# Attention in a hybrid decoder block: the product of weights and values taken by query halves, with the masked weights' high and low parts stacked

## The chip, the core and the metric

The kernel runs on one core of a Trainium2 chip. Its engines work side by side, each through its own list of instructions in order: TensorE (PE in the profile; its weight loads are listed as PEld), VectorE (DVE), ScalarE (ACT), GpSimd (POOL) and SyncE (SP, which here only issues DMA transfers; POOL issues some too). The metric is the device time of one execution, in microseconds (us).

## The reference

One residual block on a sequence of 1024 tokens and 1024 channels, float32. A normalised input is projected to query, key, value, gates and a recurrent branch; both branches are gated, projected, merged, projected once more and added to the input. Only the attention is touched here. It has 16 heads of 64 channels in 4 groups that share key and value, a window of 128 keys, and a learned sink per head:

```python
qb = q.reshape(B, nb, BLOCK, N_KV_HEADS, G, hd)        # BLOCK = 128
kb = jnp.concatenate([kp[:, :-1], kp[:, 1:]], axis=2)  # block before, own block
vb = jnp.concatenate([vp[:, :-1], vp[:, 1:]], axis=2)
diff = qi + BLOCK - kj
band = (diff >= 0) & (diff < WINDOW)                   # WINDOW = 128
s = jnp.where(mask, s, -1e30)
p = jnp.exp(s - m)
denom = jnp.sum(p, axis=-1, keepdims=True) + jnp.exp(sink - m)
o = jnp.einsum('bnkgqs,bnskd->bnqkgd', p / denom, vb)
```

A query at place q of its block sees the keys 0 to q of its own block and the keys q+1 to 127 of the block before. So for each query there is exactly one visible key at each place 0 to 127, and 128 weights hold all of a row's softmax.

## The kernel before

Float32 products are made from rounded parts: an operand is split into a high part, rounded to a shorter format (`F32R`), and a low part, the rest; high times high, high times low and low times high are summed in PSUM. A cast on ACT makes the high part, a subtraction on DVE the low one. TensorE multiplies a loaded 128x128 stationary operand with a moving operand of up to 512 columns.

**The attention works in 32 units u**: group g = u // 8, block n = u % 8, four heads of 128 queries each. One unit goes through these steps, which a loop over u (at the end of the kernel, ahead of `del W["att"]`) spreads over four rounds:

- `sink(u)`: POOL copies the four sinks into a tile `p` (three buffers) of 4 x 129 columns.
- `scores(u)` (L1330): PE, eight products of 256 columns (128 for n = 0) into `s_ps`, one buffer in PSUM.
- `maxima_a`, `maxima_d`: ACT copies the own block's scores to `p`, DVE overwrites them where the mask says so by the block before (L1345; for n = 0 POOL masks instead, L1348), and DVE takes the row maxima into `small` (L1350).
- `weights_a`, `weights_d`, one round later: ACT exponentials with their sums (L1355), DVE divides by the sums (L1361, L1362).
- `transposed`, `split_a`, `split_d`, `masks`, two rounds later: PE turns `p` to keys on partitions (`pt`, L1369), ACT casts the high part `phc` (L1374), DVE makes the low part `plc` (L1380), POOL zeroes in both the keys after the query, giving `phm` and `plm` (L1389).
- `values`, `join_a`, `join_d`, three rounds later: PE multiplies (L1403), ACT and DVE add the halves of the result into `yq` (L1412, L1413, L1423, L1424).

With w the transposed weights, v' the block before's values and v the own block's, the output is w times v' plus mask(w) times (v - v'). The stationary tile `vd` has v' (or v - v') with its high part in columns 0 to 63 and its low part in columns 64 to 127. So `values` takes four products of 512 columns: `phc` and `plc` with v', `phm` and `plm` with v - v'. A unit with n = 0 has only the first two.

**Who prepares what.** `v_prep(g)` builds these value tiles once per group, long before the attention, and stores them to DRAM (`vd_d`) with two transfers from POOL's queue. `load_v(m)` fetches them, 256 KB for two units, also from POOL's queue, into two buffers.

**What sets the order.** PE, ACT, DVE, POOL and SP run an order that the program writes out by hand. In each round PE does `scores(u)`, one piece of other work (12 products of 512 columns, from the projection of the recurrent branch: `rp`, L173, and in the first rounds the end of the input projection, `bk`, L709), `transposed(u-2)`, `values(u-3)`. ACT does the copy for `maxima_a(u)`, `weights_a(u-1)`, other casts, `split_a(u-2)`, `join_a(u-3)`. DVE follows the same pattern, with `weights_d(u-1)`, `split_d(u-2)`, `join_d(u-3)`, gating steps of finished pairs of units (L1538, L1548), the low parts of the weights of `rp` (L111). The piece of work on `rp` needs the recurrent branch's output from DRAM (`yh`, `yl`), which SP's queue fetches in the same stretch.

**Where tiles lie.** The attention's tiles are in pools on the right side of the on-chip memory that are opened one below the other: `yo` (`ob`, `yq`, and two tiles `phm`, `plm` of 2 KB in each partition), below it `pp` (a filler `pad`, three `p` of 2064 bytes, placed 2080 bytes apart, and four `small`), below it `at` (two `vd` of 2 KB, `phc`, `plc`). Within a pool, the tile asked for first lies lowest. The space was the recurrent branch's before; a tile's first use waits for whoever still reads or stores what lay there. The last such tile is `it`, the low part of the last channel block, which POOL's queue stores to `yl_d` (512 KB) as the attention begins.

Of the kernel before, what the change touches and what calls it, by code (L numbers as in the profile page):

```python
# [12 lines left out]
F32 = mybir.dt.float32  # L13
F32R = mybir.dt.float32r
# [4 lines left out]
ALU = mybir.AluOpType  # L19
# [3 lines left out]
P = 128  # L23
# [3 lines left out]
HALF = 512  # L27
NH = 16
NG = 4
# [19 lines left out]
KEEP_BUSY = 4  # L49
SLACK = 1.0, 1.3, -1.0  # L50
BANKS = (0, 1, 2, 3), (4, 5, 6, 7)


@with_exitstack
def tile_hybrid_block(ctx, tc, x, pk, rows, posr, posi, c_row, w_ss, w_gate, w_main, w_v,
                      w_g, w_ap, w_rp, w_out, out):
    nc = tc.nc
    V, A, G, T = nc.vector, nc.scalar, nc.gpsimd, nc.tensor

    def dma(dst, src, eng=nc.sync):  # L60
        dst, src = (a.bitcast(F32) if a.dtype == F32R else a for a in (dst, src))
        return eng.dma_start(dst, src)  # L62

    def f32(ap):
        return ap.bitcast(F32)
# [4 lines left out]
    def pool(st, name, bufs=1, **kw):  # L70
        return st.enter_context(tc.tile_pool(name=name, bufs=bufs, reuse_waits="tile", **kw))
# [14 lines left out]
    ident = const.tile([P, P], F32, name="ident")  # L86
# [43 lines left out]
    vd_d = [tc.dram_tile([P, 8, 2, P], F32, name=f"vd_d{g}") for g in range(NG)]  # L130
# [60 lines left out]
    with ExitStack() as st:  # L191
# [11 lines left out]
        for i in range(8):  # L203
            t = sp.tile([P, D], F32, tag="xt", name="xt", bufs=XT)
# [214 lines left out]
        def turn(n=100):  # L419
            for _ in range(n):  # L420
                if next(angle, 0) == 0:
# [10 lines left out]
                    out=bng[:], in0=pk_t[:, PK_BSC:PK_BSC + 8], scalar=1.0,  # L432
                    in1=pk_t[:, PK_NG:PK_NG + 8], op0=ALU.add, op1=ALU.mult)]}
# [133 lines left out]
    def make_operands(i):  # L567
        nl = hx.tile([P, 2, S], F32R, tag="X", name="nl")
        for a in range(2):
# [8 lines left out]
    W = {}  # L578
# [11 lines left out]
                    channel_multiplier=-1)  # L590
# [57 lines left out]
    class Load:  # L648

        pe = act = dve = 0.0  # L650
# [503 lines left out]
    def v_prep(g):  # L1154
        t = {}
        vpp = W["vpp"]

        def f0():
            t["v"] = vpp.tile([P, 8, 64], F32, tag="v32", name="v32")
            dma(t["v"][:], v_d[:, :, g, :], G)  # L1160

        def f1():
            t["d"] = vpp.tile([P, 8, 64], F32, tag="d32", name="d32")
            V.tensor_tensor(out=t["d"][:, 1:8, :], in0=t["v"][:, 1:8, :],
                            in1=t["v"][:, 0:7, :], op=ALU.subtract)
# [24 lines left out]
    def w_out_gate():  # L1190
# [88 lines left out]
    at = psx = None  # L1279
    U = {}  # L1280

    def open_attn():
        nonlocal at, psx
        psm_ctx.close()
        psx = pool(psx_ctx, "psx", space=PSUM)
        W["kq", 1] = pool(at_ctx, "kq1", side="right")
        W["yo"] = pool(at_ctx, "yo", side="right")
        W["pp"] = pool(at_ctx, "pp", bufs=3, side="right")
        W["pp"].tile([P, 72], F32, name="pad", bufs=1)
        at = pool(at_ctx, "at", side="right")  # L1290
        load_kq(1)
        load_v(0)

    def load_kq(m):
        g, t0 = m // 4, (m % 4) * 256
# [18 lines left out]

    def sink(u):
        px = U["p", u] = W["pp"].tile([P, 4, P + 1], F32, tag="p", name="p")
# [47 lines left out]

    def transposed(u):
        px = U.pop(("s", u))[1]
        pt = psx.tile([P, 4, P], F32, tag="t", name="pt")
        for j in range(4):
            W["pe"] = T.transpose(pt[:, j, :], px[:, j, 0:P], ident[:])  # L1369
        U["t", u] = [pt]  # L1370

    def split_a(u):
        phc = at.tile([P, 4, P], F32R, tag="phc", name="phc")
        A.copy(phc[:], U["t", u][0][:])  # L1374
        U["t", u].append(phc)

    def split_d(u):
        pt, phc = U.pop(("t", u))
        plc = at.tile([P, 4, P], F32R, tag="plc", name="plc")
        V.tensor_tensor(out=plc[:], in0=pt[:], in1=f32(phc[:]), op=ALU.subtract)  # L1380
        U["m", u] = phc, plc

    def masks(u):
        phc, plc = U["m", u]
        ms = []
        if u % 8:
            for s_, tag in ((phc, "phm"), (plc, "plm")):
                d_ = W["yo"].tile([P, 4, P], F32R, tag=tag, name=tag)
                G.affine_select(out=d_[:], in_=f32(s_[:]), pattern=[[0, 4], [1, P]],  # L1389
                                compare_op=ALU.is_ge, fill=0.0, base=0,  # L1390
                                channel_multiplier=-1)
                ms.append(d_)
        U["m", u] = [phc, plc], ms

    def values(u):
        n = u % 8
        vd = U["v", u // 2]
        full, masked = U.pop(("m", u))
        prods = [(vd[:, n % 2, 1 if n else 0, :], m) for m in full]
        prods += [(vd[:, n % 2, 0, :], m) for m in masked]  # L1400
        pv = psx.tile([P, 4 * P], F32, tag="v", name="pv")
        for i, (b, m) in enumerate(prods):
            W["pe"] = T.matmul(pv[:], b, m[:].rearrange("p j q -> p (j q)"),  # L1403
                               start=(i == 0), stop=(i == len(prods) - 1))
        U["pv", u] = [pv[:].rearrange("p (a e q) -> p a e q", a=2, e=2)]
        if n % 2 == 0 and u // 2 + 1 < 16:
            load_v(u // 2 + 1)

    def join_a(u):
        pvv = U["pv", u][0]  # L1410
        ob = W["yo"].tile([P, 2, P], F32, tag="ob", name="ob")
        A.copy(ob[0:64], pvv[64:128, :, 0, :])  # L1412
        A.copy(ob[64:128], pvv[0:64, :, 1, :])  # L1413
        U["pv", u].append(ob)

    def join_d(u):
        g, n = u // 8, u % 8
        pvv, ob = U.pop(("pv", u))
        if n % 2 == 0:
            W["yq"] = W["yo"].tile([P, 2, 256], F32, tag="yq", name="yq", bufs=3)  # L1420
            U["yq", u // 2] = W["yq"]
        yo = W["yq"][:, :, (n % 2) * P:(n % 2 + 1) * P]
        V.tensor_tensor(out=yo[0:64], in0=pvv[0:64, :, 0, :], in1=ob[0:64], op=ALU.add)  # L1423
        V.tensor_tensor(out=yo[64:128], in0=pvv[64:128, :, 1, :], in1=ob[64:128], op=ALU.add)  # L1424


    ps_ctx = ExitStack()
# [266 lines left out]
    for u in range(32 + 3):  # L1694
# [101 lines left out]
    for c in range(KC):  # L1796
# [24 lines left out]
        if c < 4:  # L1821
            h, l = A11[c]
# [87 lines left out]
    t_ = [tpool.tile([P, 2, 2, HALF], F32R, tag="T", name="s2") for _ in range(2)]  # L1910
# [42 lines left out]
    f = fs[:, 7, :]  # L1953

    def square_d(sl, acc):
# [17 lines left out]
                           in1=fg_bc[:, LEFT], op0=ALU.mult, op1=ALU.mult)  # L1973
# [5 lines left out]
                           in1=fg_bc[:, LEFT], op0=ALU.mult, op1=ALU.mult)  # L1979
# [80 lines left out]
```

## Time and profile before

| | |
|---|---|
| median of 3 runs | 906.73 us (906.5 to 907.61) |
| the profiled execution's own time | 907.17 us |
| its span, first to last instruction | 905.5 us |
| PE busy | 895.4 us (99%) |
| DVE busy | 717.1 us (79%) |
| ACT busy | 567.4 us (63%) |
| POOL busy | 124.7 us (14%) |
| attention on PE, first scores to last values | 557.8 to 730.1 us |
| granted clock | 0.999 |

A busy PE is not a PE at its peak: the profile's records of one product overlap with the next, so the pace of products is read from the distance between their starts. Idle time of an engine that is off the chain costs nothing. Times inside the span count from its first instruction; 1.67 us of the execution lie outside.

### The profile page before, as it was taken

To read this page: it belongs to the slowest core of one execution; us is meant where nothing else is said; L and a number is where in the kernel's file an instruction comes from. 1 tells how busy PE (TensorE), PEld (TensorE's weight loads), DVE (VectorE), ACT (ScalarE), POOL (GpSimd) and SP (SyncE) were. 2 spreads that over 40 slices of the span, in tenths; PEclk is the share of its full clock that TensorE was granted. 3 is DMA by queue.
4 is the path that set the end of the run, shared out by engine and by line. 5 is a ranking of instruction groups with operands and counts; after the bars stand their busy time and mean duration, and the time that the engine had idled before them with its cause. 6 is when DMAs were issued, how large, how long until landed. Compare 5 with 4: busy or idle time off the path is not lost.

```text
span 905.5 us, 12654 instructions
## 1 busy us (share of the span) xinstructions
PE 895.4 (99%) x4258; PEld 746.2 (82%) x4259; DVE 717.1 (79%) x1073; ACT 567.4 (63%) x1098; POOL 124.7 (14%) x216
## 2 busy tenths in 40 slices
PE   9999999999999999999999999999999999999997
PEld 6789888888888888888888888888888888888886
DVE  6987688988669875987788597999989846578855
ACT  7965554654566855786485884888888732115535
POOL 6520251200000000000000002343443300000000
PEclk9999999999999999999999999999999999999999
DMA  9829489772435353354446367996655289416604
GB/s 355 339 69 286 164 258 319 256 235 95 151 128 180 123 209 135 125 183 162 157 144 213 105 201 242 344 401 217 214 202 203 83 306 367 140 47 232 209 1 186
DMA packets 87349, 180.74 MB, mean 200 GB/s; under 512 B 8642, under 2 KB 29138, under 8 KB 87284
## 3 DMA queue, kind: packets, MB, share of 16 engines
q1 hardware_dynamic: 83200, 167.07, 52.5%
q0 software_dynamic: 3936, 12.59, 4.4%
q8 instruction: 34, 0.56, 0.3%
q14 instruction: 31, 0.25, 0.1%
q10 hardware_dynamic: 148, 0.27, 0.1%
HBM read 121.34 MB, written 58.95 MB: 199 GB/s over the span
## 4 chain that ended last, share of the span: by engine, by line
PE 52%; issue 42%; DVE 3%; ACT 2%; DMA 1%; POOL 0%; DVEq 0%; ACTq 0%; POOLq 0%
PE rp L173 14%; PE bk L709 10%; PE out L1863 6%; PE pmain L173 5%; PE s_ps L1330 3%; PE pv L1403 3%; PE pmain L485 2%; PE bk L485 2%; PE pt L1369 1%; DMA yl_d<-it 1%; PE pmain L1579 1%; PE pmain L1580 1%; PE pmain L1578 1%; ACT jk L1881 1%; PE bk L256 1%
## 5 line engine op out<-in xcount | busy, mean ns | idle before, releaser
L709 PE MATMUL bk<-nh,wh 128*128 128x512 f32 x368 | 143.4, 390 | 0.0
L709 PE MATMUL bk<-nl,wh 128*128 128x512 f32 x368 | 143.3, 389 | 0.0
L709 PE MATMUL bk<-nh,wl 128*128 128x512 f32 x368 | 98.4, 389 | 0.0
L111 DVE TENSOR_TENSOR wl<-r,wh 128x512 fp32r<-128x512 f32 x109 | 74.8, 692 | 23.3 <-ACT wh L105 23.2
L105 ACT CAST wh<-r 128x512 fp32r<-128x512 f32 x107 | 65.6, 618 | 32.1 <-PE rp L173 11.8
L709 PEld LDWEIGHTS bk<-nh,wl 128*128 128x128 f32 x368 | 69.1, 188 | 14.3
L709 PEld LDWEIGHTS bk<-nh,wh 128*128 128x128 f32 x368 | 69.2, 188 | 14.2
L709 PEld LDWEIGHTS bk<-nl,wh 128*128 128x128 f32 x368 | 69.1, 188 | 14.1
L709 PE MATMUL bk<-hh,wh 128*128 128x512 f32 x184 | 71.7, 390 | 0.0
L709 PE MATMUL bk<-hl,wh 128*128 128x512 f32 x184 | 71.6, 389 | 0.0
L111 DVE TENSOR_TENSOR wl<-ws,wh 128x512 fp32r<-128x512 f32 x76 | 52.1, 686 | 7.2 <-ACT wh L105 7.1
L62 POOL DMA_DIRECT2D yh_d<-av x1 | 0.6, 567 | 371.9 <-ACT av L1092 371.9
L1355 ACT ACTIVATE p<-p,small 128x129 f32<-128x129 f32 x128 | 50.0, 396 | 0.0
L709 PE MATMUL bk<-hh,wl 128*128 128x512 f32 x184 | 49.2, 389 | 0.0
L105 ACT CAST wh<-ws 128x512 fp32r<-128x512 f32 x76 | 46.0, 614 | 4.8 <-DVE ws L731 2.4
L709 PEld LDWEIGHTS bk<-hh,wl 128*128 128x128 f32 x184 | 34.6, 188 | 7.1
L709 PEld LDWEIGHTS bk<-hh,wh 128*128 128x128 f32 x184 | 34.6, 188 | 7.1
L709 PEld LDWEIGHTS bk<-hl,wh 128*128 128x128 f32 x184 | 34.6, 188 | 7.1
L1330 PEld LDWEIGHTS s_ps<-ks,qs 128*128 128x128 f32 x256 | 34.1, 189 | 4.4 <-DVE p L1345 2.0
L1330 PE MATMUL s_ps<-ks,qs 128*128 128x256 f32 (+1 forms) x256 | 35.6, 282 | 0.3 <-DVE p L1345 0.2
L709 PE MATMUL bk<-hha,wh 128*128 128x512 f32 x92 | 35.8, 390 | 0.0
L709 PE MATMUL bk<-hla,wh 128*128 128x512 f32 x92 | 35.8, 389 | 0.0
(378 smaller groups left out, 2293.1 us busy)
## 6 DMA issues: line engine op xcount, KB each, us to landing
r<-w_main SPq DMA_DIRECT2D x100, 256.0 KB, 4.2
wada<-w_ss SPq DMA_DIRECT2D x16, 512.0 KB, 9.0
qs<-q_d SPq DMA_DIRECT2D x16, 512.0 KB, 5.2
wo_d<-wr SPq DMA_DIRECT2D x28, 256.0 KB, 3.1
wo<-wo_d SPq DMA_DIRECT2D x14, 512.0 KB, 5.6
ks<-k_d SPq DMA_DIRECT2D x12, 384.0 KB, 4.3
xt<-x SPq DMA_DIRECT2D x8, 512.0 KB, 7.1
sma_d<-c SPq DMA_DIRECT2D x16, 256.0 KB, 4.4
```

The costliest lines, as they stand in the source:

```text
L105: A.copy(dst[0][:], src)
L111: V.tensor_tensor(out=dst[1][:], in0=src, in1=f32(dst[0][:]), op=ALU.subtract)
L173: mm = T.matmul(ps[hf], ww, xx[kc][hf], start=(kc == 0 and ww is w_h and xx is xh), stop=(kc == KC - 1 and xx is xl))
L256: T.matmul(bk[i % 2], zero[:, 0:P], zero, start=True, stop=True)
L485: T.matmul(starts[c][hf], ww[:, c0:c0 + P], xh[kc][hf], start=(kc == 0 and t_ == "h"), stop=(kc == KC - 1 and t_ == "l"))
L709: W["pe"] = T.matmul(ps, ww[:, kc * P:(kc + 1) * P], b[kc][i], start=(first and n == 0), stop=(n == 11), skip_group_check=not first)
L1330: W["pe"] = T.matmul(o, qs[:, j, qc], ks[:, kb:n % 2 + 2, b, :], start=(b == 0), stop=(b == 1))
L1355: A.activation(px[:, j, :], px[:, j, :], AF.Exp, bias=sm[:, 0, j:j + 1], accum_out=sm[:, 1, j:j + 1])
L1369: W["pe"] = T.transpose(pt[:, j, :], px[:, j, 0:P], ident[:])
L1403: W["pe"] = T.matmul(pv[:], b, m[:].rearrange("p j q -> p (j q)"), start=(i == 0), stop=(i == len(prods) - 1))
L1578: T.matmul(o, hh[kc][th][:, ts_], wh[:, cols], start=(kc == 0), stop=False)
L1863: T.matmul(o, a[k][x_][:, p * P:(p + 1) * P], b[k][y_][:, cols], start=(first and k == 0 and i == 0), stop=(k == 3 and i == 2), skip_group ...
```

## The change

By halves of 64 queries, the mask gets smaller. For queries 0 to 63, the keys 64 to 127 of the own block are always masked; for queries 64 to 127, the keys 0 to 63 are never masked. So:

- the transposed weights are laid out by query half, then head (`p l j q`); the transposes write two runs of 64 columns each;
- for half 0 the plain product uses v'; for half 1 its stationary tile has v in the rows of keys 0 to 63 and v' in those of keys 64 to 127;
- only 64 keys are left under the mask in either half. Their high part takes 64 partitions of a tile `pm`, their low part the other 64, against a stationary tile that has v - v' of these keys twice;
- `values` takes three products of 256 columns per half, six in all, for four of 512 (units with n = 0 keep their two of 512);
- `masks` makes four POOL instructions of 64 partitions x 256 columns for two of 128 x 512, two of which move data to the other 64 partitions;
- `v_prep` stores more and in smaller parts: eight transfers per group for two, some 1.9 MB for 0.96 MB; `load_v` now fetches 256 KB for each unit, two units ahead, into three buffers;
- one tile `pm` takes the place of `phm` and `plm`; the joins read and write runs of 64 columns for runs of 128.

```diff
@@ v_prep, f3
-            dma(vd_d[g][:, 1:8, 1, :], t["vs"][:, 0:7, :], G)
-            dma(vd_d[g][:, :, 0, :], t["dv"][:], G)
+            o, vs, dv = vd_d[g], t["vs"], t["dv"]
+            dma(o[:, 1:8, 0, 0, :], vs[:, 0:7, :], G)
+            dma(o[:, 0, 0, 0, :], vs[:, 0, :], G)
+            dma(o[TOP, 1:8, 1, 0, :], vs[TOP, 1:8, :], G)
+            dma(o[END, 1:8, 1, 0, :], vs[END, 0:7, :], G)
+            for l, half_ in enumerate((TOP, END)):
+                for to in (TOP, END):
+                    dma(o[to, 1:8, l, 1, :], dv[half_, 1:8, :], G)
@@ open_attn
         load_v(0)
+        load_v(1)
@@
-    def load_v(m):
-        g, n0 = m // 4, (m % 4) * 2
-        vd = at.tile([P, 2, 2, P], F32R, tag="vd", name="vd", bufs=2)
-        if n0:
-            dma(vd[:], vd_d[g][:, n0:n0 + 2, :, :], G)
+    def load_v(u):
+        g, n = u // 8, u % 8
+        vd = U["v", u] = at.tile([P, 2, 2, P], F32R, tag="vd", name="vd", bufs=3)
+        if n:
+            dma(vd[:], vd_d[g][:, n, :, :, :], G)
         else:
-            dma(vd[:, 0, 0, :], vd_d[g][:, 0, 0, :], G)
-            dma(vd[:, 1, :, :], vd_d[g][:, 1, :, :], G)
-        U["v", m] = vd
+            dma(vd[:, 0, 0, :], vd_d[g][:, 0, 0, 0, :], G)
@@ transposed
-        pt = psx.tile([P, 4, P], F32, tag="t", name="pt")
+        pt = psx.tile([P, 2, 4, 64], F32, tag="t", name="pt")
         for j in range(4):
-            W["pe"] = T.transpose(pt[:, j, :], px[:, j, 0:P], ident[:])
+            W["pe"] = T.transpose(pt[:, :, j, :], px[:, j, 0:P], ident[:])
@@ masks
-            for s_, tag in ((phc, "phm"), (plc, "plm")):
-                d_ = W["yo"].tile([P, 4, P], F32R, tag=tag, name=tag)
-                G.affine_select(out=d_[:], in_=f32(s_[:]), pattern=[[0, 4], [1, P]],
-                                compare_op=ALU.is_ge, fill=0.0, base=0,
-                                channel_multiplier=-1)
+            pm = W["yo"].tile([P, HALF], F32R, tag="pm", name="pm")
+            lo, hi = slice(0, 256), slice(256, HALF)
+            for to, s_, from_, cols in ((TOP, phc, TOP, lo), (END, phc, END, hi),
+                                        (END, plc, TOP, lo), (TOP, plc, END, hi)):
+                G.affine_select(out=pm[to, cols], in_=f32(s_[from_, cols]),
+                                pattern=[[0, 4], [1, 64]], compare_op=ALU.is_ge, fill=0.0,
+                                base=0, channel_multiplier=-1)
@@ values
-        prods = [(vd[:, n % 2, 1 if n else 0, :], m) for m in full]
-        prods += [(vd[:, n % 2, 0, :], m) for m in masked]
-        for i, (b, m) in enumerate(prods):
-            W["pe"] = T.matmul(pv[:], b, m[:].rearrange("p j q -> p (j q)"),
-                               start=(i == 0), stop=(i == len(prods) - 1))
+        for l in range(2 if n else 1):
+            cols = slice(l * 256, l * 256 + 256) if n else slice(0, HALF)
+            for i, t_ in enumerate(m):
+                W["pe"] = T.matmul(pv[:, cols], vd[:, l, i // 2, :], t_[:, cols],
+                                   start=(i == 0), stop=(i == len(m) - 1))
@@
-        if n % 2 == 0 and u // 2 + 1 < 16:
-            load_v(u // 2 + 1)
+        if u + 2 < 32:
+            load_v(u + 2)
@@ join_a, join_d (operands in runs of 64, same elements)
-        A.copy(ob[0:64], pvv[64:128, :, 0, :])
+        A.copy(ob[0:64], pvv[64:128, :, :, 0, :])
...
```

More of the change, by code (lines that the diff above doesn't have):

```diff
@@ L51 @@
 BANKS = (0, 1, 2, 3), (4, 5, 6, 7)
+TOP, END = slice(0, 64), slice(64, 128)
 @with_exitstack
@@ L129, in tile_hybrid_block @@
     v_d = tc.dram_tile([P, 8, NG, 64], F32, name="v_d")
-    vd_d = [tc.dram_tile([P, 8, 2, P], F32, name=f"vd_d{g}") for g in range(NG)]
+    vd_d = [tc.dram_tile([P, 8, 2, 2, P], F32, name=f"vd_d{g}") for g in range(NG)]
     q_d = [tc.dram_tile([4, 512, 256], F32, name=f"q_d{g}") for g in range(NG)]
@@ L1366, in transposed @@
         px = U.pop(("s", u))[1]
-        pt = psx.tile([P, 4, P], F32, tag="t", name="pt")
+        pt = psx.tile([P, 2, 4, 64], F32, tag="t", name="pt")
         for j in range(4):
-            W["pe"] = T.transpose(pt[:, j, :], px[:, j, 0:P], ident[:])
-        U["t", u] = [pt]
+            W["pe"] = T.transpose(pt[:, :, j, :], px[:, j, 0:P], ident[:])
+        U["t", u] = [pt[:].rearrange("p l j q -> p (l j q)")]
     def split_a(u):
-        phc = at.tile([P, 4, P], F32R, tag="phc", name="phc")
-        A.copy(phc[:], U["t", u][0][:])
+        phc = at.tile([P, HALF], F32R, tag="phc", name="phc")
+        A.copy(phc[:], U["t", u][0])
         U["t", u].append(phc)
@@ L1378, in split_d @@
         pt, phc = U.pop(("t", u))
-        plc = at.tile([P, 4, P], F32R, tag="plc", name="plc")
-        V.tensor_tensor(out=plc[:], in0=pt[:], in1=f32(phc[:]), op=ALU.subtract)
+        plc = at.tile([P, HALF], F32R, tag="plc", name="plc")
+        V.tensor_tensor(out=plc[:], in0=pt, in1=f32(phc[:]), op=ALU.subtract)
         U["m", u] = phc, plc
@@ L1395, in values @@
+            lo, hi = slice(0, 256), slice(256, HALF)
[4 more added lines that the diff above has]
+                                base=0, channel_multiplier=-1)
+            U["m", u] = phc, plc, pm
     def values(u):
@@ L1396, in values @@
         n = u % 8
-        vd = U["v", u // 2]
-        full, masked = U.pop(("m", u))
-        prods = [(vd[:, n % 2, 1 if n else 0, :], m) for m in full]
-        prods += [(vd[:, n % 2, 0, :], m) for m in masked]
+        vd = U.pop(("v", u))
+        m = U.pop(("m", u))
         pv = psx.tile([P, 4 * P], F32, tag="v", name="pv")
-        for i, (b, m) in enumerate(prods):
-            W["pe"] = T.matmul(pv[:], b, m[:].rearrange("p j q -> p (j q)"),
-                               start=(i == 0), stop=(i == len(prods) - 1))
@@ L1409, in join_a @@
+        if u + 2 < 32:
+            load_v(u + 2)
     def join_a(u):
         pvv = U["pv", u][0]
-        ob = W["yo"].tile([P, 2, P], F32, tag="ob", name="ob")
-        A.copy(ob[0:64], pvv[64:128, :, 0, :])
-        A.copy(ob[64:128], pvv[0:64, :, 1, :])
+        ob = W["yo"].tile([P, 2, 2, 64], F32, tag="ob", name="ob")
+        A.copy(ob[0:64], pvv[64:128, :, :, 0, :])
+        A.copy(ob[64:128], pvv[0:64, :, :, 1, :])
         U["pv", u].append(ob)
@@ L1421, in join_d @@
             U["yq", u // 2] = W["yq"]
-        yo = W["yq"][:, :, (n % 2) * P:(n % 2 + 1) * P]
-        V.tensor_tensor(out=yo[0:64], in0=pvv[0:64, :, 0, :], in1=ob[0:64], op=ALU.add)
-        V.tensor_tensor(out=yo[64:128], in0=pvv[64:128, :, 1, :], in1=ob[64:128], op=ALU.add)
+        yo = W["yq"][:, :, (n % 2) * P:(n % 2 + 1) * P].rearrange("p a (l q) -> p l a q", l=2)
+        V.tensor_tensor(out=yo[0:64], in0=pvv[0:64, :, :, 0, :], in1=ob[0:64], op=ALU.add)
+        V.tensor_tensor(out=yo[64:128], in0=pvv[64:128, :, :, 1, :], in1=ob[64:128], op=ALU.add)
     ps_ctx = ExitStack()
```

5 lines of the change are left out of this document (1 added, 4 removed).

## The prediction

> **What bounds the kernel now.** I read the busy times first, then the engines by stretches of the span, then instruction by instruction where the units of attention run. Busy times:
>
> ```profile
> span 905.5 us, 12654 instructions
> PE 895.4 (99%) x4258; PEld 746.2 (82%) x4259; DVE 717.1 (79%) x1073; ACT 567.4 (63%) x1098; POOL 124.7 (14%) x216
> ```
>
> PE sets the end, so what counts is what a round of the attention costs on PE, and who is just behind it. The stretches (columns: length, then busy time and instructions of PE, PEld, DVE, ACT, POOL, clock, DMA share, GB/s):
>
> ```profile
> 600.00:620.00 20.00, 19.91 (x110) 16.51 (x110) 19.11 (x36) 16.99 (x55) 6.42 (x13) 1.00 0.94 358
> 620.00:640.00 20.00, 20.00 (x112) 16.92 (x112) 19.28 (x36) 16.54 (x54) 8.52 (x15) 1.00 0.57 193
> 640.00:660.00 20.00, 20.00 (x113) 17.18 (x112) 18.01 (x34) 17.10 (x54) 7.55 (x13) 1.00 0.63 209
> ...
> 740.00:760.00 20.00, 20.00 (x90) 16.58 (x89) 11.25 (x13) 5.83 (x8) 0.00 (x0) 1.00 1.04 398
> ```
>
> PE is full everywhere, but from 600 to 640 DVE is at 96% as well, and from 640 at 90%. After the attention DVE is at 56%: what PE gains is then kept to the end. And PE does wait for DVE; the waits of PE's weight loads between 560 and 640 are
>
> ```profile
> PEld s_ps L1330 <- DVE p L1345: 2.0, 5, 0.7
> ```
>
> 2.0 us in five waits, all scores waiting for the masked copy (L1345) to leave `s_ps`.
>
> **The products: what is saved on PE.** One round's products (start, duration, instruction):
>
> ```profile
> 640.39 1.10 PE L1330 MATMUL s_ps<-ks,qs 128*128 128x256 f32 x8
> ...
> 644.08 0.60 PE L1369 MATMUL pt<-ident,p 128*128 128x128 f32 x4
> 644.44 0.48 PE L1403 MATMUL pv<-phc,vd 128*128 128x512 f32 x1
> ...
> 645.22 0.39 PE L1403 MATMUL pv<-plm,vd 128*128 128x512 f32 x1
> 645.45 1.11 PE L1330 MATMUL s_ps<-ks,qs 128*128 128x256 f32 x8
> 646.40 0.63 PE L173 MATMUL rp<-hha,wh 128*128 128x512 f32 x2
> ```
>
> A round takes 645.45 - 640.39 = 5.06 us. The last of four products takes 645.45 - 645.22 = 0.23 us of PE, the four 1.01, so 0.26 for the first three on average, the first with the handover from the transposes; I take 0.235 each, 0.94. Products of 256 columns: the eight scores take 646.40 - 645.45 = 0.95, 0.119 each. The scores use each stationary tile twice in a row; the early product of v does not, and loads one each time:
>
> ```profile
> 69.72 0.28 PE L1579 MATMUL pmain<-wl,hha 128*128 128x256 f32 x1
> ...
> 71.88 0.28 PE L1579 MATMUL pmain<-wl,hh 128*128 128x256 f32 x1
> ...
> L1579 PEld LDWEIGHTS pmain<-wl,hha x16: 188/192/193, 68.5 to 76.8; 128*128 128x128 f32 x16
> ```
>
> 18 intervals in 2.16 us: 0.12 each, although one load's record lasts 0.192. So six products cost 6 x 0.12 = 0.72, and a unit saves 0.94 - 0.72 = 0.22. There are 28 units with n > 0: 6.2 us if all of it were kept.
>
> The Trainium skill, "TensorE: Matmul & The Clock Gate", Part 3, "The mechanism", says that weight loads overlap running products only when the row group differs. By that rule a unit pays two more loads in full; estimated from the load's record here, 2 x 0.192 - 0.22 = 0.16 slower per unit. The 0.12 pace above, with a load per product, contradicts it.
>
> **Where DVE limits, nothing is saved.** The masked copies of three rounds in a row, and the low parts of weights from 575 to 715 us (count, then busy time, mean ns):
>
> ```profile
> 619.06 0.75 DVE L1345 COPY_PREDICATED p<-mgt,s_ps 128x512 f32<-128x512 uint32 x1
> ...
> 624.35 0.74 DVE L1345 COPY_PREDICATED p<-mgt,s_ps 128x512 f32<-128x512 uint32 x1
> ...
> 628.81 0.74 DVE L1345 COPY_PREDICATED p<-mgt,s_ps 128x512 f32<-128x512 uint32 x1
> ...
> L111 DVE TENSOR_TENSOR wl<-r,wh 128x512 fp32r<-128x512 f32 x16 | 11.1, 694 | 0.0
> ```
>
> A round of DVE back to back takes 628.81 - 624.35 = 4.46 us, and 5.29 where it also makes a low part (L111). 16 of these in 28 rounds: 4.46 + 16 / 28 x 0.69 = 4.85 on average, less 0.09 since one round in eight has no masked copy (0.74). PE's round of 5.06 would be 4.84. So DVE's work fits by a hair. In the rounds between about 590 and 630 it does not: four of the five waits lie there (the fifth is at 565.62, shown below), and a faster PE only waits longer. They hold seven of the 28 units. After 630 there are 18 (values of units 12 to 31 without 16 and 24): 18 x 0.22 = 4.0, less 0.4 for rounds with L111 in which DVE runs out of its lead. The first three units save 0.7 ahead of the dense stretch; DVE's waits in that time come half from PE's chain, so I keep half, 0.35.
>
> **The wait that comes in at the start.** Tiles in `yo` shrink by 2 KB, so `pp` moves up by 2048 bytes; `at` grows by as much. The `p` buffers lie 2080 bytes apart: the first now lies where the second lay, but for 32 bytes. Who waits there now (POOL, DVE, ACT, PE; in brackets idle time and its end):
>
> ```profile
> 554.00 0.55 POOL L62 DMA_DIRECT2D yl_d<-it  x1 [1.81 <-DVE it L1096]
> ...
> 555.62 1.73 POOL L1318 COPY p<-pk_t 128x4 f32<-128x4 f32 x1
> ...
> 562.42 0.31 POOL L1318 COPY p<-pk_t 128x4 f32<-128x4 f32 x2 [2.18 <-DMA yl_d<-it]
> 562.42 0.69 DVE L1350 TENSOR_REDUCE small<-p 128x4 f32<-128x516 f32 x1 [5.12 <-DMA yl_d<-it]
> ...
> 558.94 0.59 ACT L1339 COPY p<-s_ps 128x512 f32<-128x512 f32 x1 [2.38 <-PE s_ps L1330]
> ...
> 561.51 1.11 PE L1330 MATMUL s_ps<-ks,qs 128*128 128x256 f32 x8
> ...
> 565.62 1.21 PE L1330 MATMUL s_ps<-ks,qs 128*128 128x256 f32 x8 [0.24 <-DVE p L1345]
> ```
>
> The first `p` is free at 555.62, the second only when the store of `it` has landed, at 562.4. In the new layout the first one waits too, and ACT's copy of unit 0's scores with it: 562.4 to 563.0 for 558.94. The scores of unit 1 need that copy done, since `s_ps` has one buffer: 563.0 for 561.51, 1.5 us of PE idle. Behind the copy on ACT stand a weight cast and a bank copy, each wanted several us later. Then POOL's mask (0.64) and DVE's maxima follow at 563.7 for 562.42, and the scores of unit 2 come at about 567.0 for 565.62. I take +1.4. If ACT did not have to wait, 0; if DVE's lost 1.3 us are also paid again, +2.7. `small` moves off this tile, which helps nobody while `p` waits.
>
> **Masks, loads and the preparation, each costed at nothing.**
>
> ```profile
> L1389 POOL TENSOR_SCALAR_AFFINE_SELECT plm<-plc x28: 628/632/643, 575.9 to 727.3; 128x512 fp32r<-128x512 f32 x28
> ...
> L589 POOL TENSOR_SCALAR_AFFINE_SELECT mf<-mf x1: 390/390/390, 53.2 to 53.2; 128x128 f32<-128x128 f32 x1
> ...
> L62 POOL DMA_DIRECT2D vd<-vd_d x20: 537/554/567, 554.5 to 711.9; - x20
> ```
>
> A mask of 256 columns lies between 0.39 (128 columns) and 0.63: four take 1.6 to 2.5 us for 1.26. I take 0.45 each, nearer the short one. With one load (0.55) and the sink copy POOL needs under 3 us of a 4.85 us round, and the product needs the masks a round later; cover gone, a late mask costs PE its lateness. The waiting mask keeps the next load and sink behind it on POOL; both are wanted rounds later. `phc` is now read until the fourth of six products, not the first: ACT's next split starts up to 0.24 us later, covered by DVE's lead. Transposes in runs of 64, the joins and the splits move the same elements; bounds 0 and, for the transposes, 0.03 x 128 = 3.8 us if one took a 256-column product's 0.12 for its 0.09 ((644.44 - 644.08) / 4). I take 0.
>
> The loads double, 128 to 256 KB a unit, when DMA is full (0.94 above). By 606 that is six units' extra 128 KB, 0.75 MB, 2 us at 358 GB/s. The tightest load there:
>
> ```profile
> 606.58 0.32 SPq L62 DMA_DIRECT2D yl<-yl_d  x1
> yl<-yl_d SPq DMA_DIRECT2D x1, 512.0 KB, 9.9
> 618.04 0.62 PE L173 MATMUL rp<-yl,wh 128*128 128x512 f32 x2
> ```
>
> It lands at 616.5 and is used at 618.04, 1.5 us of cover; PE comes there about 1 us later than now (start wait less the first savings), so 2 us just fit. Bounds 0 and +2.
>
> The preparation issues six more transfers per group:
>
> ```profile
> L62 POOL DMA_DIRECT2D vd_d<-vs x4: 968/968/1136, 124.4 to 177.8; - x4
> 134.80 0.61 DVE L1164 TENSOR_TENSOR d<-v 128x448 f32<-128x448 f32 x1
> 139.87 0.39 PE L709 MATMUL bk<-hh,wl 128*128 128x512 f32 x1
> ```
>
> At 0.55 to 0.97 each the next group's load moves back by some 4 us on POOL's queue, and L1164 at 134.80 may wait 1 to 3 us for it. The low part made right after it (end 136.1) is used at 139.87: 3.8 us of cover. I take 0, bound +1.
>
> **Sum.** +1.4 - 0.35 - 4.0 + 0.4 = -2.5 us. The profiled execution's 907.17 (span 905.5 and 1.67 around it) becomes 904.6; it stood 0.4 above the median of 906.73, which becomes 904.2. Own range of this case 902.7 to 905.6.
>
> **Rivals.**
> 1. *All of it kept.* DVE runs far enough ahead, and the wait at the start is swallowed by the DVE-bound stretch: 906.7 - 6.2 + 0 to 1.4, 900.5 to 902. For it: only 2.0 us of waits so far. Against: DVE's 96%.
> 2. *Eaten by DVE.* DVE's mean round comes to 4.9 to 5.0 (the 4.85 with stretches), against PE's 5.06: that leaves 0.06 to 0.16 in the 18 units, 1 to 3 us, less the 1.4: 905 to 907.
> 3. *Slower: POOL holds up DVE.* Place: DVE's steps with two operands in on-chip memory (L1362, L1538, L1548). Rows:
>
> ```profile
> L1362 DVE TENSOR_TENSOR p<-p,small x32: 691/693/1094, 567.1 to 719.7; 128x512 f32<-128x512 f32 x32
> 595.32 0.63 POOL L1389 TENSOR_SCALAR_AFFINE_SELECT phm<-phc 128x512 fp32r<-128x512 f32 x1 [1.11 <-ACT phc L1374]
> 595.39 1.09 DVE L1362 TENSOR_TENSOR p<-p,small 128x512 f32<-128x512 f32 x1
> ```
>
> The step that began 0.07 us into a mask took 1.09 for 0.69. With four masks a round for two, one more such hit costs 0.4 of DVE per unit, more than PE's 0.22: 28 x (0.4 - 0.22) = +5, 911.8. It decides once DVE loses over 0.3 a unit. Against: shorter masks, so shorter hits.
> The Trainium skill, "SBUF — State Buffer", "SBUF: two separate sides", says the pair of ports is an exclusive lock between such DVE steps and GpSimd steps that read; the two rows agree.
> 4. *Slower: weight loads in the open.* Two more loads of 0.192 per unit unhidden: 28 x 0.16 = +4.6, 911.3. The 0.12 pace speaks against it.
>
> **Chances.** Forecast 0.47, rival 1 0.15, rival 2 0.24, rival 3 0.10, rival 4 0.04. 0.2% (1.8 us) is about what a measurement of this kernel tells from no change: faster below 904.9. The forecast is faster in 0.37 of its 0.47, rival 1 always, rival 2 in 0.04 and otherwise the same: faster 0.56, same 0.30, slower 0.14. Range: down into rival 1 and up past rival 2, with a late load: 900.8 to 908.2.
>
> **What would show it.** The six products' starts 0.12 apart; the scores of unit 1 near 563 with ACT's first copy released by the store of `it`; waits for the masked copy over 2.0 us; rounds of 4.85 after 630. Wrong if rounds stay at 5.07, if L1362 has a mean well over 0.73, or if the first copy of `p` does not wait.

## The result and the profile after

The changed kernel takes 918.9 us at the median of 4 runs (915.41 to 923.01); the kernel before, run beside it, 906.89 (906.5 to 907.61). The ratio is 1.0133, with a 95% interval of 1.009 to 1.0176. The forecast was 904.2, faster, with a range up to 908.2. The profiled execution of the changed kernel took 923.01 us, 4.1 above its median, so what its stalls add up to below is that much more than in a typical run.

TensorE no longer fills the span. From the page of the changed kernel (span; engines; then the queue that POOL issues to: packets, MB, share of the time of the 16 DMA engines):

```profile
span 921.0 us, 12879 instructions
PE 895.7 (97%) x4314; PEld 747.8 (81%) x4315; DVE 716.3 (78%) x1073; ACT 567.9 (62%) x1098; POOL 158.5 (17%) x308
...
q0 software_dynamic: 6496, 19.94, 7.7%
```

PE is as busy as before, to 0.3 us (895.4), and stands idle for 15 us more. The same queue row before:

```profile
q0 software_dynamic: 3936, 12.59, 4.4%
```

Where the idle time lies is seen in stretches of 10 us (length, then busy time and instructions of PE, PEld, DVE, ACT, POOL, PE's granted clock, DMA share, GB/s). Two of the kernel before, where PE is full from 120 to 200 us:

```profile
140.00:150.00 10.00, 10.00 (x46) 8.29 (x45) 8.31 (x12) 4.75 (x9) 1.00 (x2) 1.00 0.97 324
150.00:160.00 10.00, 10.00 (x46) 8.29 (x45) 7.70 (x11) 4.14 (x8) 0.00 (x0) 1.00 0.91 308
```

The changed kernel, the same view, with the sum over 120 to 200 us:

```profile
150.00:160.00 10.00, 9.72 (x43) 7.70 (x41) 5.05 (x7) 3.71 (x7) 2.04 (x3) 1.00 0.98 258
160.00:170.00 10.00, 1.59 (x4) 1.30 (x5) 2.49 (x3) 1.01 (x2) 0.00 (x0) 0.62 0.82 275
170.00:180.00 10.00, 10.00 (x41) 8.14 (x40) 9.52 (x14) 3.55 (x7) 4.11 (x6) 0.87 0.81 263
180.00:190.00 10.00, 7.67 (x27) 5.86 (x26) 7.32 (x13) 5.95 (x12) 2.80 (x5) 0.83 0.79 204
...
sum 80.00, PE 65.92 PEld 53.27 DVE 53.96 ACT 34.74 POOL 27.60; mean PE 8.24 PEld 6.66 DVE 6.75 ACT 4.34 POOL 3.45
```

This is the stretch in which `v_prep` stores the tiles of `v`, 370 us ahead of the attention. PE is idle there for 80 - 65.92 = 14.1 us. The first scores come 18.5 us later, at 576.4 us for 557.8. The other 4.4 us are an estimate of what PE loses to a lower granted clock after the gaps: 27 matmuls take 7.67 us from 180 on, 0.28 each, where before 46 take 10, 0.22 each. In stretches of 5 us, the lowest clock stands at the end of the longest gap:

```profile
165.00:170.00 5.00, 1.59 (x4) 1.30 (x5) 2.49 (x3) 1.01 (x2) 0.00 (x0) 0.50 0.69 255
```

From the first scores to the end of the span the changed kernel takes 921.0 - 576.4 = 344.6 us, where before it took 905.5 - 557.8 = 347.7. So the attention and what follows gained 3.1 us, and the preparation lost 18.5.

What the engines waited for between 95 and 240 us in the changed kernel (us in total, times, longest):

```profile
DVE gate_bc L1212 <- DMA wr<-w_gate: 12.9, 2, 11.4
...
PE bk L710 <- DVE wl L114: 8.7, 1, 8.7
...
DVE d L1165 <- DMA v<-v_d: 6.8, 1, 6.8
```

In the kernel before, no wait of DVE for `v` of that size stands there, and the one for `w_gate` is short:

```profile
DVE gate_bc L1205 <- DMA wr<-w_gate: 2.5, 2, 1.3
```

And the instructions behind it, from the timeline of the changed kernel (start, duration; in brackets idle time and its end):

```profile
124.45 3.20 POOL L63 DMA_DIRECT2D vd_d<-vs  x4
127.64 2.88 POOL L63 DMA_DIRECT2D vd_d<-dv  x4
130.52 0.92 POOL L63 DMA_DIRECT2D v<-v_d  x1
...
141.72 0.62 DVE L1165 TENSOR_TENSOR d<-v 128x448 f32<-128x448 f32 x1 [6.82 <-DMA v<-v_d]
...
151.48 1.18 SPq L63 DMA_DIRECT2D wr<-w_gate  x1
...
166.47 1.28 DVE L1212 SCALAR_TENSOR_TENSOR gate_bc<-wr,pk_t,gate_bc 128x1024 f32<-128x1024 f32 x1 [11.42 <-DMA wr<-w_gate]
```

DVE stands twice at the head of its queue before an operand that has not landed: 6.8 us for `v`, 11.4 us for a row block of `w_gate`. Behind it in the queue wait the sums of weights (L732); ACT's casts wait for the sums, DVE's low parts for the casts, and PE for those. The second of these transfers has nothing to do with `v`: it is on SP's queue, and the stretches around it have the DMA engines at 0.98 and 0.82. Issued at 151.48, it landed 14.9 us later; before, the loads of `w_gate` in this part landed within 5.2. The load of `v`, issued at 130.52, took 11 us, where before such loads took 6.1 to 8.2.

### The profile page after: what moved, and what is told of

It reads as the page before. It is cut to its first block, busy times and chain, and to the rows that moved or that the text cites. A ratio compares the mean times of both kernels' runs of the same rounds, so it can differ in the third digit from the quotient of the medians.

```text
span 921.0 us, 12879 instructions
## 1 busy us (share of the span) xinstructions
PE 895.7 (97%) x4314; PEld 747.8 (81%) x4315; DVE 716.3 (78%) x1073; ACT 567.9 (62%) x1098; POOL 158.5 (17%) x308
## 3 DMA queue, kind: packets, MB, share of 16 engines
q0 software_dynamic: 6496, 19.94, 7.7%
## 4 chain that ended last, share of the span: by engine, by line
issue 42%; PE 40%; DVE 5%; DMA 4%; ACT 4%; POOL 4%; SPq 1%; DVEq 0%; ACTq 0%; POOLq 0%
PE rp L174 13%; PE bk L710 5%; PE out L1869 4%; PE pmain L174 4%; PE s_ps L1336 3%; PE pmain L486 2%; PE bk L486 2%; PE pv L1409 2%; POOL vd_d L63 2%; DMA wo<-wo_d 1%; PE pt L1375 1%; DMA v<-v_d 1%; POOL lam_p L1142 1%; DMA wr<-w_gate 1%; DMA yl_d<-it 1%
## 5 line engine op out<-in xcount | busy, mean ns | idle before, releaser
L1396 POOL TENSOR_SCALAR_AFFINE_SELECT pm<-phc 64x256 fp32r<-64x256 f32 x56 | 31.6, 564 | 30.7 <-ACT phc L1380 25.0
```

The source lines that it names most:

```text
L1396: G.affine_select(out=pm[to, cols], in_=f32(s_[from_, cols]), pattern=[[0, 4], [1, 64]], compare_op=ALU.is_ge, fill=0.0, base=0, channel_m ...
```

## The experiments

**1. The stores alone.** The kernel before, attention untouched, with four more stores of 64 partitions per group to a buffer that nobody reads.

```diff
...
             dma(vd_d[g][:, :, 0, :], t["dv"][:], G)
+            for l, half_ in enumerate((TOP, END)):
+                for to in (TOP, END):
+                    dma(more_d[g][to, 1:8, l, :], t["dv"][half_, 1:8, :], G)
```

> The kernel before, its attention untouched, with four more stores per group in v_prep: the low and high halves of the difference tile, 64 partitions and 224 KB each, to a buffer that nothing reads, so that a group stores 1856 KB as in the changed kernel (960 KB before), in six transfers where that has eight. Theory 1 (the loss is made by the stores of v_prep, between 130 and 195 us): slower by most of the 15 to 18 us that the changed kernel loses ahead of the first scores, so 917 to 925 us, with TensorE idle and its clock below 0.9 between 160 and 190 us. Theory 2 (the stores are hidden and the loss belongs to what the attention does with its loads and masks): 906 to 908 us, no idle TensorE in that stretch.

Measured: 917.7 us (917.11 to 918.77) against 907.42; ratio 1.0116, interval 1.0102 to 1.013. The stores alone bring 10.3 us, with the attention of before, and the same two waits of DVE:

```profile
DVE gate_bc L1210 <- DMA wr<-w_gate: 10.3, 2, 8.9
...
DVE d L1166 <- DMA v<-v_d: 4.5, 1, 4.5
```

That is not the whole loss of the preparation. The changed kernel is 12.0 us slower at the median although its attention gains some 3.1 (run 2), so its preparation loses about 15. This run makes two thirds of that. It issues six stores per group, four of them of 64 partitions, where the changed kernel issues eight, six of them of 64 partitions; no run separates what the rest is.

**2. The attention alone.** The changed kernel with the two stores of before. It leaves out the stacked tiles: the products of the second query half read other rows, so this run is good for its time only.

```diff
-            dma(o[:, 1:8, 0, 0, :], vs[:, 0:7, :], G)
...
+            dma(vd_d[g][:, 1:8, 1, :], t["vs"][:, 0:7, :], G)
+            dma(vd_d[g][:, :, 0, :], t["dv"][:], G)
...
-            dma(vd[:], vd_d[g][:, n, :, :, :], G)
+        n0 = min(n, 6)
...
+            dma(vd[:], vd_d[g][:, n0:n0 + 2, :, :], G)
```

> The changed kernel with the two stores per group of before, into a buffer of before's size. Each unit still loads 256 KB in one transfer, but reads the rows of another layout, so the products of the second query half get the wrong values; all instructions and sizes of the attention are those of the changed kernel. This leaves the change of the attention alone. Theory 1 (stores): the stretch up to 560 us runs as before and the attention gains about 3 us as the profile of the changed kernel shows from the first scores on: 903 to 905 us. Theory 2 (attention): stays slower than before, 910 to 919 us.

Measured: 904.3 us (903.89 to 906.11), ratio 0.9969, interval 0.9958 to 0.9981. That is the time that the prediction gave to the whole change, 904.2. PE is busy throughout from 120 to 220 us. Theory 1 holds, and the prediction's steps for the attention can be read in this run. The scores, the products and the waits of PE's weight loads from 540 to 760 us:

```profile
L1331 PE MATMUL s_ps<-ks,qs x256: 220/283/387, 557.9 to 708.2; 128*128 128x256 f32 x112, 128*128 128x128 f32 x16
L1404 PE MATMUL pv<-phc,vd x60: 277/360/481, 574.4 to 725.9; 128*128 128x256 f32 x56, 128*128 128x512 f32 x4
L1404 PE MATMUL pv<-pm,vd x56: 278/280/300, 579.3 to 726.2; 128*128 128x256 f32 x56
...
PEld s_ps L1331 <- DVE p L1346: 1.6, 6, 0.4
```

POOL's masks of the high and low parts, and DVE's multiplication by the reciprocals (count, then busy time, mean ns, idle time before):

```profile
L1391 POOL TENSOR_SCALAR_AFFINE_SELECT pm<-phc 64x256 fp32r<-64x256 f32 x56 | 31.6, 565 | 30.6 <-ACT phc L1375 24.9 <-PE s_ps L1331 3.8
L1391 POOL TENSOR_SCALAR_AFFINE_SELECT pm<-plc 64x256 fp32r<-64x256 f32 x56 | 23.6, 421 | 9.9 <-DVE plc L1381 7.3
...
L1363 DVE TENSOR_TENSOR p<-p,small 128x512 f32<-128x512 f32 x32 | 23.3, 729 | 1.1
```

One round of it, and the start of the attention (timeline):

```profile
561.56 0.59 ACT L1340 COPY p<-s_ps 128x512 f32<-128x512 f32 x1 [5.56 <-DMA yl_d<-it]
562.20 1.22 PE L1331 MATMUL s_ps<-ks,qs 128*128 128x256 f32 x8 [0.41 <-ACT p L1340]
...
643.61 0.36 PE L1404 MATMUL pv<-phc,vd 128*128 128x256 f32 x1
643.81 0.28 PE L1404 MATMUL pv<-plc,vd 128*128 128x256 f32 x1
...
644.28 0.28 PE L1404 MATMUL pv<-pm,vd 128*128 128x256 f32 x1
644.41 1.12 PE L1331 MATMUL s_ps<-ks,qs 128*128 128x256 f32 x8
...
649.26 1.12 PE L1331 MATMUL s_ps<-ks,qs 128*128 128x256 f32 x8
```

The six products take 644.41 - 643.61 = 0.80 us where four took 1.01, and this round 649.26 - 644.41 = 4.85 where one took 5.07 (650.52 - 645.45).

**3. The doubling in the loads.** Two stores per group, and five loads of 64 partitions per unit on SP's queue (the expectation says four; it is two for the stacked half and three for the rest, 140 in all; the four units with n = 0 keep their one load on POOL's queue).

```diff
...
+            halves = o[:, n, 0, :].rearrange("(l p) c -> p l c", l=2)
+            dma(vd[TOP, :, 0, :], o[TOP, n:n + 2, 1, :])
+            for l in range(2):
+                dma(vd[END, l, 0, :], o[END, n, 1, :])
+            for to in (TOP, END):
+                dma(vd[to, :, 1, :], halves)
```

> The changed kernel with two stores per group (1024 KB, the last block's values included) and the doubling moved to the loads: four loads of 64 partitions per unit on SP's queue put the stacked tile together, so the output is that of the reference. Theory 1 (stores): 903 to 905 us, faster than before by 2 to 4 us, unless 124 loads in place of 28 hold up SP's other loads, which would show as waits for qs, ks, r or wo in the attention and bring it to 906 to 909. Theory 2 (attention): 910 to 919 us.

Measured: 916.53 us (915.0 to 920.04), ratio 1.0118, interval 1.0099 to 1.0137. The number lies in the range of theory 2, but for neither theory's reason: the preparation is mended (PE is busy throughout from 120 to 550 us), and a new stall, made by this run's own loads, stands in the attention. PE's waits, and SP's issues around 607 us:

```profile
PE pv L1409 <- DMA vd<-vd_d: 2.5, 2, 2.1
PE rp L174 <- DMA yl<-yl_d: 2.0, 3, 0.8
...
607.07 0.33 SPq L63 DMA_DIRECT2D yl<-yl_d  x1
609.30 0.81 SPq L63 DMA_DIRECT2D r<-w_rp  x2
610.21 3.18 SPq L63 DMA_DIRECT2D vd<-vd_d  x5
```

Five small loads hold SP's queue for 3.18 us, 0.64 each, twice what the load of 512 KB ahead of them takes (0.33), and the loads that PE wants next queue behind them (0.60 is the median of all 140). From 600 to 650 us PE is busy for 45.0 of 50 us.

**4. The same, with the buffers of `p` back in their old place** (`plc` moves to the pool `yo`).

> As the run before it in this list, and the tile plc lies in the pool yo in place of at, which moves the three buffers of p down by 2 KB to where they lay before, so that the first of them doesn't overlap it, whose store the first sink waited for. If that wait of some 5 us on the first p costs the 1.4 us that the prediction gave it: 1.0 to 1.8 us below the run before it, 901.5 to 903.5 us, and no wait for the store of it at the first p. If the wait was hidden: the same time as that run within 0.5 us.

Measured: 916.06 us (915.12 to 919.26), ratio 1.0102, interval 1.0085 to 1.0119; the two can't be told apart. The first `p` no longer waits, but the same store now holds up `small`, as it did before the change (5.1 us there):

```profile
DVE small L1356 <- DMA yl_d<-it: 4.4, 1, 4.4
```

With the stall of run 3 still in it, this run can't tell what the first wait is worth; run 6 tells more.

**5. The doubling moved behind the preparation.** Two stores per group (1024 KB, with the last block's values), and five copies per group from DRAM to DRAM, meant for slots 48 to 143 of the order that is written out by hand, some 220 to 490 us.

```diff
...
+        for i, (to, from_) in enumerate((
+                (o[TOP, 1:8, 1, 0, :], o[TOP, 2:9, 0, 0, :]),
+                (o[END, 1:8, 1, 0, :], o[END, 1:8, 0, 0, :]),
+                (o[END, 1:8, 1, 1, :], o[END, 1:8, 0, 1, :]),
+                (o[TOP, 1:8, 1, 1, :], o[END, 1:8, 0, 1, :]),
+                (o[END, 1:8, 0, 1, :], o[TOP, 1:8, 0, 1, :]))):
+            at_slot(48 + 25 * g + 5 * i, ("N", 0, 0, lambda to=to, from_=from_: dma(to, from_, G)))
```

> The changed kernel with two stores per group in v_prep (1024 KB), and the doubling made by five copies per group from DRAM to DRAM, 224 KB each on POOL's queue, spread over the slots 48 to 143 (some 220 to 490 us), where the DMA engines of the kernel before are busy 0.40 to 0.51 of the time. The attention is that of the changed kernel and the output that of the reference. Theory 1 (a burst of stores beside the other transfers of 130 to 195 us is the loss): 903.5 to 905.5 us, as in the run with two stores (904.3). Rival (the bytes themselves cost, wherever they lie: 7 MB of copies, each byte read and written, slow the loads of w_main): 907 to 915 us, with waits of ACT for DMA r<-w_main between 220 and 490 us.

Measured: 903.27 us (902.76 to 904.14), ratio 0.9957, interval 0.9944 to 0.9969. It is faster than both kernels. The copies did not run where they were meant to. A slot is a place in the order and not a time: POOL ran ahead and issued all twenty right behind the last stores of `v_prep`:

```profile
L63 POOL DMA_DIRECT2D vd_d<-vd_d x20: 697/698/745, 179.8 to 220.3; - x20
L63 POOL DMA_DIRECT2D vd_d<-vs x4: 885/890/976, 122.7 to 178.1; - x4
```

Two stretches of the kernel before (the last two columns are the DMA share and GB/s), then the same two of this run:

```profile
180.00:190.00 10.00, 10.00 (x46) 8.29 (x45) 9.84 (x17) 5.81 (x11) 0.00 (x0) 1.00 0.53 162
200.00:210.00 10.00, 10.00 (x46) 8.29 (x45) 8.97 (x13) 4.13 (x8) 0.00 (x0) 1.00 0.45 164
```

```profile
180.00:190.00 10.00, 10.00 (x46) 8.29 (x45) 9.84 (x17) 5.98 (x11) 2.78 (x5) 1.00 0.89 259
200.00:210.00 10.00, 10.00 (x46) 8.29 (x45) 8.32 (x11) 4.34 (x7) 3.46 (x5) 1.00 0.99 369
```

The sum of its stretches from 120 to 210 us, its queue and its copies:

```profile
sum 90.00, PE 90.00 PEld 74.58 DVE 77.10 ACT 48.49 POOL 21.95; mean PE 10.00 PEld 8.29 DVE 8.57 ACT 5.39 POOL 2.44
...
q0 software_dynamic: 6688, 21.12, 7.3%
...
vd_d<-vd_d POOLq DMA_DIRECT2D x20, 224.0 KB, 6.1
```

Its queue moves more than the changed kernel's (21.12 MB for 19.94), and PE does not miss a beat up to 560 us. So the doubling costs nothing between 180 and 221 us, where it brings the DMA share from 0.35 to 0.95 up to 0.84 to 1.00, while the extra stores, in four bursts between 125 and 202, cost 10 us and more. A DMA share near 1 is thus not by itself a loss. What is different behind 180 us is argued and not tested: the last loads of `v` and `w_gate` are issued by then (162.5 and 156.8), and before the change that stretch has room.

**6. The same, without the wait at the start** (`plc` in `yo`, the first `small` at the bottom of `pp`).

> As the run before it in this list, with plc in the pool yo and the first small tile at the bottom of pp, so that neither the first p nor small overlaps the tile it, whose store to yl_d both kernels wait for in the first unit (5.1 us of DVE before, 5.6 us of ACT with the change and two stores). If that wait is on the path: 1 to 3 us below the run before it. If it only pushes work into slack: within 0.5 us.

Measured: 902.84 us (901.92 to 902.93), ratio 0.9948, interval 0.9935 to 0.996: 0.4 us less, with intervals that overlap. The fastest median of the study. The wait is worth at most a few tenths here.

**7. The same bytes in whole tiles.** The kernel before with two more stores of 128 partitions, so that run 1 and this one store equal bytes.

```diff
...
+            for l in range(2):
+                dma(more_d[g][:, 1:8, l, :], t["dv"][:, 1:8, :], G)
```

> The kernel before with two more stores per group of 128 partitions and 448 KB each to a buffer that nothing reads: 1856 KB per group in four transfers, where the first run of this study had the same bytes in six, four of them of 64 partitions (917.7 us). If the bytes cost: 915 to 919 us. If the transfers of 64 partitions or their number cost: 907 to 911 us.

Measured: 912.82 us (911.64 to 914.14), ratio 1.0055, interval 1.004 to 1.0071. It falls between the two expectations: of the 10.3 us of run 1 the bytes bring 5.5, and the rest comes with the halves, of which there are twice as many (sixteen more transfers for eight); shape and number are not told apart. The queue's rows, this run and then run 1:

```profile
q0 software_dynamic: 4960, 16.27, 5.8%
```

```profile
q0 software_dynamic: 5216, 16.27, 6.6%
```

The DMA engines' time for the extra 3.7 MB: 5.8% of 912.4 us less 4.4% of 905.5 us, times 16, is 210 us in whole tiles, and 6.6% of 915.9 less the same, times 16, is 330 us in halves: 1.6 times as much for the same bytes (1.4 to 1.8, since the shares are rounded).

**8. The order on POOL's queue.** The changed kernel, each next group's load of `v` ahead of the stores.

```diff
...
+        if g + 1 < NG:
+            waiting[1].append([("S", 0, 0, steps_[g + 1][0])])
+        waiting[1].append([("D", 0, 1.38, f3)])
```

> The changed kernel, with each next group's load of v issued on POOL's queue ahead of the eight stores of the group (v32 has two buffers for it). This takes away the 6.8 us wait of L1165 for v, the step that the prediction costed at nothing. If the loss is that order on one queue: 905 to 909 us. If it is the DMA engines filled by the stores, the loads of w_gate and w_main late by it: 911 to 917 us, and the wait of gate_bc for DMA wr<-w_gate stays near 11 us.

Measured: 915.24 us (914.24 to 920.84), ratio 1.0099, interval 1.0074 to 1.0125. The wait for `v` is gone, the other stays:

```profile
DVE gate_bc L1211 <- DMA wr<-w_gate: 11.9, 2, 10.5
```

**9. More time for `w_gate`.** The changed kernel with three slots more between a load of `w_gate` and its step, and, as a control, the kernel before with the same slots.

```diff
...
-                idle.append(load(k + 2))
+                idle.extend([load(k + 2), slots(3)])
```

> The changed kernel, stores as they are, with three slots (8 us) more between each load of w_gate and the step of gate_bc that uses it, so that gate_bc doesn't stand at the head of DVE's queue while its operand is under way. If the loss passes through that wait (11.4 us of DVE, and behind it the sums, the casts and the low parts that TensorE wants): 907 to 912 us, with TensorE's idle time at 150 to 175 us gone but that behind v still there. If the loads of w_main and the stores of q_d and sma_d are late by themselves: 914 to 919 us, the idle time staying with other waits.

> The kernel before with the same slots, to see what they cost by themselves: 905.5 to 908 us, the same as before, if the list of idle work has room for 65 us of delay; more if work of it is left over behind the attention.

Measured: 910.96 us (907.68 to 915.91), ratio 1.0048, interval 1.0024 to 1.0071; the control 907.47 us, ratio 1.0005, interval 0.9996 to 1.0015. With three slots more, some 8 of the 12 us lost are back. That wait is gone, and the other has grown:

```profile
DVE d L1165 <- DMA v<-v_d: 13.0, 2, 9.3
```

**10. Both at once.**

> The changed kernel, stores and their bytes as they are, with both edits at once: each next group's load of v ahead of the stores, and three slots more between a load of w_gate and its step. If the whole loss is DVE standing at the head of its queue before operands that the stores make late: 903.5 to 906 us, as with two stores (904.3), and no wait of DVE above 3 us for v or wr before 240 us. If the stores cost the other transfers too: 908 us or more, with waits for w_main, q_d or sma_d in their place.

Measured: 912.88 us (908.93 to 913.96), ratio 1.0051, interval 1.0034 to 1.0068, no better than run 9 alone. DVE's waits from 95 to 240 us:

```profile
DVE rlo L637 <- DMA q_d<-rlo: 5.7, 1, 5.7
DVE ws L732 <- DMA r<-w_main: 4.9, 1, 4.9
```

Neither `v` nor `w_gate` is among them; now a store of `q` that must free its buffer and a weight of the main products are late. As long as the burst stays where it is, mending one wait hands its place to the next transfer in the line. Of these runs, only making the burst smaller (run 2) or moving part of it (run 5) removes the loss.

## Why the prediction was wrong

**The step that failed is the preparation, "I take 0, bound +1".** In its place stand 18.5 us in the profiled execution, about 15 at the median. The step priced six more transfers by their issue on POOL's queue, some 4 us, and looked for one late operand, `v` (L1164 in the kernel before, L1165 now). The issue was priced rightly: the load of `v` went out 4.1 us later (130.52 for 126.38). What failed is that a transfer was taken to land nearly as fast as before. Three things were missing.

1. *The bytes.* A group stores 1856 KB for 960, and the stretches of before have the DMA engines at 0.97 and 0.91 there. The step looked at a queue, while the engines under all queues had little room; the prediction read the DMA share for the loads of the attention, but not here. The bytes alone cost 5.5 us (run 7). Run 5 shows it from the other side: from 120 to 230 us POOL's queue takes 28.0% of the DMA engines' time there, for 14.8% before, and nothing is lost, with the copies from 180 us on; run 7 takes 26.7%, with its stores in four bursts from 125 to 189 us, and loses the 5.5.
2. *The shape.* Stores in halves of 64 partitions cost 1.6 times the engine time of whole ones (runs 1 and 7). The Trainium skill, "DMA: Bandwidth & Descriptors", "Rules for kernel authors", says that two transfers to disjoint halves of the partitions bring nothing, since both share the same engines, and to use one of 128 partitions. The runs go further: halves, twice as many, cost 4.8 us more here (10.3 against 5.5).
3. *The other customers.* The first wait was 6.8 us where the step had 1 to 3. The larger one, 11.4 us, was a load of `w_gate` on SP's queue that the change doesn't touch. Its step on DVE is filler that could have come some slots later (the control of run 9 loses nothing by it), but it stood ahead of the sums that PE needs.

On top of these came about 4 us of PE at a lower granted clock after the gaps, 0.62 in the stretch from 160 to 170 us and 0.50 in its second half. The Trainium skill, "TensorE: Matmul & The Clock Gate", Part 1, "What's actually happening", gives an idle PE half its clock after an idle window; the stretches agree: 0.50 from 165 to 170 us, and from 190 on 1.00 again.

**The attention, step by step**, read in run 2 against before:

- *Products.* A unit was to save 0.94 - 0.72 = 0.22. It saves 1.01 - 0.80 = 0.21, with the last five 0.12 apart, and the rounds from unit 13 on take 4.86 on average for 5.02 before (4.85 were forecast). Rival 4, weight loads in the open, falls.
- *DVE limits until 630.* Half right. The scores of unit 13 come at 619.87 before and at 619.89 in run 2, with starts at 557.8 and 557.9: nothing saved by then, though eight units had made the smaller products, some 1.7 us. Of these, 0.6 went to the start, and the rest was lost in the rounds between (the longest, from unit 7 to unit 8, takes 5.45 for 5.05). But the sign that was named, waits for the masked copy over 2.0 us, did not come: they are 1.6 in six, for 2.0 in five before. That DVE alone took these savings is argued and not shown. From unit 13 on the rounds save, but for the two whose unit has n = 0: by the last scores 18 rounds gain 3.0 us (710.31 to 707.34).
- *The wait at the start.* The mechanism is right: ACT's first copy waits for the store of `it`. The size was +1.4 and the scores of unit 1 are 0.7 later (562.20 for 561.51), 0.6 with the later start taken off. The store had landed by 561.56, not 562.4, and the rounds up to unit 13 swallow the 0.6. That part is rival 1's; the gain of 6.2 is not.
- *Masks.* 0.45 each was estimated; the groups of run 2 give 0.42 for the low part and 0.57 for the high part, 2.0 us a unit for 1.26 before, and no wait on POOL reaches PE. DVE's multiplication by the reciprocals has a mean of 729 ns for 724: rival 3, the port, falls.
- *Loads.* No wait of PE for `yl` in run 2: 0, as taken.

From the first scores to the last product the sum is 726.2 - 557.9 = 168.3 for 729.7 - 557.8 = 171.9, 3.6 us less, of which 3.1 reach the end of the span (902.4 for 905.5). The forecast was 2.5. That it came so near is partly luck: at unit 15, at 630 us, run 2 is 0.4 ahead (629.91 for 630.32) where the forecast had it 1.05 behind; from there to the last product it gains 3.1 for 3.6; and 0.4 is lost again behind the attention, which the forecast had at nothing. None of these decided the sign. The term taken at 0 with a bound of 1 did.

## What to carry to other kernels

A change is paid for wherever its data are made, not only where they are used: price the bytes of every store that it adds against the DMA share of the stretch where the store runs, and not only its place in a queue. When the share stands above 0.9, any transfer may be the one that comes late, so look through every in-order queue for cheap work that waits for a load and has urgent work behind it. If the layout has to be doubled, move the doubling to a stretch where the DMA engines have room and no load is urgent, as run 5 does; that made of a loss of 12 us a gain of 4. And look in the trace where moved work really ran: a place in an engine's order is not a time.

## What the runs showed of the hardware that was not expected

- Stores of 64 partitions took 1.6 times the DMA engines' time per byte of stores of 128 (330 and 210 us for 3.7 MB, in runs 1 and 7, beside the other transfers of 120 to 200 us).
- Loads of 32 and 64 KB took SP 0.64 us each to issue in a run of five, twice the 0.33 of a load of 512 KB; many small loads held up the queue that issued them while the DMA engines were at 0.85 (600 to 650 us of run 3).
- Copies from DRAM to DRAM (20 of 224 KB, 6.1 us each to landing) beside a stream of weight loads cost no time that a measurement shows, from 180 to 221 us, where the DMA engines were at 0.35 to 0.95 without them and at 0.84 to 1.00 with them.
- A six-product unit with a weight load of 0.19 us ahead of each product runs at 0.12 us per product: the loads are hidden behind products of the same full array.
